# Low part of every second FFN weight chunk: an adding DMA onto a negated high part, in place of a VectorE subtraction

## The chip, the cores and the metric

The kernel runs on one core of one Trainium2 chip. The metric is the device time of one execution in microseconds (us). The engines are TensorE (PE, with its weight loads PEld), VectorE (DVE), ScalarE (ACT), GpSimd (POOL) and SyncE (SP); transfers run on 16 DMA engines that all queues share. Times of single steps come from one profiled execution, in which "L184" means line 184 of the kernel.

## What is computed

One decoder layer over 256 tokens of width 2048: a gated recurrent branch and a stick-breaking attention branch, merged, then a SwiGLU feed-forward block (FFN) and a gated per-layer embedding. The change touches only the weights of the FFN, the middle lines here:

```python
x = x + mix @ w_o
h = rmsnorm(x, g_ffn)
g, u = split(h @ w_ffn_gu, 2)          # w_ffn_gu: 2048 x 11264
x = x + (silu(g) * u) @ w_ffn_down     # w_ffn_down: 5632 x 2048
x = x + sigmoid(rmsnorm(x, g_ple) @ w_ple_gate) * (p @ w_ple_proj)
```

All values are float32. TensorE multiplies float32r, a shortened format, so every operand is carried as a high part, rounded to float32r, and a low part, the remainder. A product is high x high + high x low + low x high.

## The kernel before, in words

**Weights as a stream.** All weight matrices are packed in the order of use (`PLAN`) and cut into 690 chunks of at most eight 128x128 tiles; a full chunk is 128 x 1024 floats, 512 KB. `Stream` moves them through three stages. `dma_to` (L167) loads chunk j from device memory into one of four `w32` buffers, issued from SP. `split_to` makes the parts: ScalarE copies `w32` into `whi` (L183, rounding to float32r), VectorE subtracts `whi` from `w32` into `wlo` (L184). `whi` and `wlo` have four buffers each, so chunk j can be split only when TensorE has finished chunk j-4. `need` keeps the split three chunks ahead of the use and the loads four further.

**Use.** `dense` multiplies a block of chunks. A `wide` matmul (L366) takes a tile of `whi` against 512 columns, the activations' high and low parts side by side; a `low` matmul (L370) takes a tile of `wlo` against 256 columns, the high parts. In each chunk all eight of one kind run and then all eight of the other: low first in odd places of a block and in its last chunk, wide first in the others.

**The FFN.** Chunks 382 to 653, 272 of 690. `gu(q)` takes for each pair of rows a block of four chunks for the gate and four for the up projection; `dense_sum` adds the two column halves (ScalarE, then VectorE), a scaling, Silu and a product follow, and `split` writes the result's parts (L256 on ScalarE, L250 on VectorE). `down(q)` uses blocks of three chunks of six to eight tiles and adds into the residual on VectorE. The order is gu, gu, down, gu, down, gu, down, down. After the first block of the FFN and after the first of the last stage, a sum over all ones (L419) gives the norm.

**Order.** The program text gives every engine's instructions, and a list scheduler, which has a timeline of its own, decides the order in which they stand in each engine's queue. Each engine takes its queue strictly in order and waits at an instruction whose inputs or buffers aren't there yet.

Of the kernel before, what the change touches and what calls it, by code (L numbers as in the profile page):

```python
# [8 lines left out]
F32 = mybir.dt.float32  # L9
F32R = mybir.dt.float32r  # L10
AF = mybir.ActivationFunctionType
ALU = mybir.AluOpType

P = 128
# [111 lines left out]
PLAN = plan()  # L126
# [10 lines left out]
OFFS = []  # L137
# [11 lines left out]
class Stream:  # L149
# [23 lines left out]
    def split_to(self, n):  # L173
        n = min(n, len(CHUNKS))
        self.dma_to(n)
        while self.n_split < n:
            j = self.n_split
            i, a, b = CHUNKS[j]
            t = self.raw.pop(j)
            c = P * (b - a)  # L180
            hi = self.phl.tile([P, 1024], F32R, tag="whi", name=f"whi_{j}")
            lo = self.phl.tile([P, 1024], F32R, tag="wlo", name=f"wlo_{j}")
            self.hi_ins = self.nc.scalar.activation(hi[:, :c], t[:, :c], AF.Copy)  # L183
            self.lo_ins = self.nc.vector.tensor_tensor(lo[:, :c], t[:, :c], hi[:, :c].bitcast(F32), ALU.subtract)  # L184
            res = self.parts.setdefault(i, [])
            for x in range(b - a):
                s = slice(x * P, (x + 1) * P)
                res.append((hi[:, s], lo[:, s], hi, lo, x * P))
            self.n_split += 1
# [715 lines left out]
```

## Time and profile before

| | |
|---|---|
| Median of 3 runs (lowest to highest) | 1933.47 us (1933.33 to 1933.83) |
| The profiled execution, its own time | 1933.27 us |
| Its span, first to last instruction | 1931.5 us |
| Granted TensorE clock, mean | 0.999 |
| VectorE, ScalarE, share of the span | 67%, 57% |
| Read from device memory | 357.68 MB, 186 GB/s over the span |

The span is the stretch that the trace covers; the execution's own time is 1.8 us longer. "Busy" is time in which an engine works on an instruction; matmuls overlap, so TensorE's own busy time says that it never stood still, and the starts of its runs tell how long they really take. "Idle before" and the waits name what an engine stood still for.

### The profile page before, as it was taken

To read this page: it belongs to the slowest core of one execution; us is meant where nothing else is said; L and a number is where in the kernel's file an instruction comes from. 1 tells how busy PE (TensorE), PEld (TensorE's weight loads), DVE (VectorE), ACT (ScalarE), POOL (GpSimd) and SP (SyncE) were. 2 spreads that over 40 slices of the span, in tenths; PEclk is the share of its full clock that TensorE was granted. 3 is DMA by queue.
4 is the path that set the end of the run, shared out by engine and by line. 5 is a ranking of instruction groups with operands and counts; after the bars stand their busy time and mean duration, and the time that the engine had idled before them with its cause. 6 is when DMAs were issued, how large, how long until landed. Compare 5 with 4: busy or idle time off the path is not lost.

```text
span 1931.5 us, 28549 instructions
## 1 busy us (share of the span) xinstructions
PE 1923.7 (100%) x11126; PEld 1702.5 (88%) x11126; DVE 1293.2 (67%) x1848; ACT 1109.2 (57%) x1504; POOL 1.8 (0%) x8
## 2 busy tenths in 40 slices
PE   9999999999999999999999999999999999999998
PEld 8889889988888888888888888888888888888888
DVE  8787778665567777765666666666566665666775
ACT  7787778854466667674454544444344444444553
POOL 0000000000000000000000000000000000000000
PEclk9999999999999999999999999999999999999999
DMA  6556565566655555556666566666666566665664
GB/s 245 194 183 198 177 201 173 187 199 191 198 176 171 169 163 154 175 173 200 202 210 189 182 196 187 187 194 187 193 188 186 178 201 190 188 198 175 196 205 133
DMA packets 104391, 361.64 MB, mean 187 GB/s; under 512 B 11584, under 2 KB 13760, under 8 KB 104256
## 3 DMA queue, kind: packets, MB, share of 16 engines
q1 hardware_dynamic: 104112, 359.71, 58.8%
q8 instruction: 87, 1.43, 0.3%
q14 instruction: 48, 0.39, 0.1%
q10 hardware_dynamic: 144, 0.12, 0.0%
HBM read 357.68 MB, written 2.10 MB: 186 GB/s over the span
## 4 chain that ended last, share of the span: by engine, by line
PE 99%; ACT 1%; DVE 0%; issue 0%; ACTq 0%
PE ps L366 58%; PE ps L370 30%; PE ps L622 2%; PE ps L621 2%; PE ps L620 2%; PE ps L348 1%; PE ps L350 1%; PE ps L349 1%; PE ps L338 0%; PE ps L451 0%; ACT whi L183 0%; ACT T L256 0%; PE ps L602 0%; PE ps L601 0%; PE ps L339 0%; PE ps L419 0%
## 5 line engine op out<-in xcount | busy, mean ns | idle before, releaser
L184 DVE TENSOR_TENSOR wlo<-w,whi 128x1024 fp32r<-128x1024 f32 (+4 forms) x690 | 824.1, 1197 | 426.8 <-ACT whi L183 421.3
L183 ACT ACTIVATE whi<-w 128x1024 fp32r<-128x1024 f32 (+4 forms) x690 | 713.6, 1037 | 507.2 <-PE ps L366 373.8
L366 PE MATMUL ps<-B,whi 128*128 128x512 f32 x2528 | 611.0, 391 | 0.0
L366 PE MATMUL ps<-A,whi 128*128 128x512 f32 x2400 | 585.6, 391 | 0.0
L366 PEld LDWEIGHTS ps<-B,whi 128*128 128x128 f32 x2528 | 464.0, 188 | 89.1
L366 PEld LDWEIGHTS ps<-A,whi 128*128 128x128 f32 x2400 | 438.6, 188 | 83.3
L370 PEld LDWEIGHTS ps<-B,wlo 128*128 128x128 f32 x2528 | 325.9, 191 | 13.1
L370 PE MATMUL ps<-B,wlo 128*128 128x256 f32 x2528 | 330.1, 283 | 0.0
L370 PEld LDWEIGHTS ps<-A,wlo 128*128 128x128 f32 x2400 | 312.5, 191 | 14.4 <-DVE wlo L184 1.2
L370 PE MATMUL ps<-A,wlo 128*128 128x256 f32 x2400 | 320.0, 283 | 0.8 <-DVE wlo L184 0.8
L256 ACT ACTIVATE T<-ps 128x256 f32<-128x256 f32 x242 | 79.3, 380 | 209.6 <-PE ps L366 209.6
L250 DVE TENSOR_TENSOR T<-ps,T 128x256 f32<-128x256 f32 x242 | 92.0, 419 | 129.6 <-ACT T L256 129.5
L256 ACT ACT_TABLE_LOAD x65 | 83.4, 1283 | 5.1 <-DVE ze L250 2.7
L256 ACT ACTIVATE T<-T 128x512 f32<-128x512 f32 (+2 forms) x116 | 69.7, 602 | 20.9 <-DVE T L250 20.0
L250 DVE TENSOR_TENSOR T<-T,rstd 128x256 f32<-128x256 f32 x194 | 75.0, 418 | 2.5 <-ACT rstd L256 2.3
L250 DVE TENSOR_TENSOR C<-ps,C 128x256 f32<-128x256 f32 x176 | 63.1, 417 | 15.1 <-PE ps L366 13.4
L250 DVE TENSOR_TENSOR T<-T,T 128x512 f32<-128x512 f32 (+2 forms) x109 | 70.3, 646 | 2.5 <-ACT T L256 2.2
L622 PE MATMUL ps<-whi,A 128*128 128x512 f32 x128 | 49.8, 389 | 0.0
L621 PE MATMUL ps<-wlo,A 128*128 128x512 f32 x128 | 49.8, 389 | 0.0
L620 PE MATMUL ps<-whi,A 128*128 128x512 f32 x128 | 48.9, 389 | 0.0
L253 DVE SCALAR_TENSOR_TENSOR T<-T,prm_sb,T 128x255 f32<-128x255 f32 (+3 forms) x74 | 34.6, 507 | 8.0 <-ACT T L256 7.9
L348 PE MATMUL ps<-X,whi 128*128 128x256 f32 x140 | 39.6, 283 | 0.0
(138 smaller groups left out, 868.5 us busy)
## 6 DMA issues: line engine op xcount, KB each, us to landing
w<-in_w_dram SPq DMA_DIRECT2D x588, 512.0 KB, 3.7
w<-in_w_dram SPq DMA_DIRECT2D x80, 448.0 KB, 3.4
w<-in_w_dram SPq DMA_DIRECT2D x16, 384.0 KB, 3.0
C<-in_xT_dram SPq DMA_DIRECT2D x16, 256.0 KB, 4.0
out_dram<-T SPq DMA_DIRECT2D x16, 128.0 KB, 3.8
w<-in_w_dram SPq DMA_DIRECT2D x4, 320.0 KB, 3.4
w<-in_w_dram SPq DMA_DIRECT2D x2, 256.0 KB, 4.2
T<-in_pT_dram SPq DMA_DIRECT2D x1, 256.0 KB, 4.7
```

What stands on the lines that cost most here:

```text
L183: self.hi_ins = self.nc.scalar.activation(hi[:, :c], t[:, :c], AF.Copy)
L184: self.lo_ins = self.nc.vector.tensor_tensor(lo[:, :c], t[:, :c], hi[:, :c].bitcast(F32), ALU.subtract)
L250: nc.vector.tensor_tensor(o, a, b, op)
L253: nc.vector.scalar_tensor_tensor(o, a, s, b, op0, op1)
L256: nc.scalar.activation(o, i, f, **kw)
L348: nc.tensor.matmul(o, wt[0], xh, start=start, stop=False)
L349: nc.tensor.matmul(o, wt[0], xl, start=False, stop=False)
L366: nc.tensor.matmul(pss[e], wt[0], rhs(xs, k), start=(k == 0), stop=(k == n - 1))
L370: nc.tensor.matmul(pss[e][:, :256], wt[1], rhs(xs, k)[:, :256], start=False, stop=False)
L620: nc.tensor.matmul(ps, xh, wh, start=(k == 0), stop=False)
L621: nc.tensor.matmul(ps, xh, wl, start=False, stop=False)
L622: nc.tensor.matmul(ps, xl, wh, start=False, stop=(k == KD - 1))
```

## The change

For FFN chunks (`gu`, `dn`) with an odd number, 136 of the 272, `wlo` is made in two steps instead of one. ScalarE writes the negated high part into `wlo` (L186), and a DMA issued from GpSimd (L187) reads the chunk's weights a second time from device memory and adds them in place. VectorE's subtraction (L184 before, L189 after) remains for the other chunks.

```diff
             self.hi_ins = self.nc.scalar.activation(hi[:, :c], t[:, :c], AF.Copy)
-            self.lo_ins = self.nc.vector.tensor_tensor(lo[:, :c], t[:, :c], hi[:, :c].bitcast(F32), ALU.subtract)
+            if PLAN[i][0][0] in ("gu", "dn") and j % 2:
+                src = self.w[OFFS[j]:OFFS[j] + P * c].rearrange("(p c) -> p c", p=P)
+                self.nc.scalar.activation(lo[:, :c], hi[:, :c].bitcast(F32), AF.Copy, scale=-1.0)
+                self.nc.gpsimd.dma_start(lo[:, :c], src, accum_op=ALU.add)
+            else:
+                self.lo_ins = self.nc.vector.tensor_tensor(lo[:, :c], t[:, :c],
+                                                           hi[:, :c].bitcast(F32), ALU.subtract)
```

Queue by queue, the built program has 136 instructions fewer on VectorE, 136 copies more on ScalarE (and one table load more), and 136 DMAs on GpSimd, whose queue held nothing in this part before. SP's queue is the same, instruction by instruction. Up to the FFN all queues agree.

From chunk 383 on the scheduler also orders TensorE's and ScalarE's work anew. In a stretch of `gu`, which repeats every eight chunks, TensorE's order is this (hi396 is the eight wide matmuls of chunk 396, lo396 its eight low ones, "hi402 x4" four of them):

```
before: hi396 lo396 | lo397 hi397 | hi398 lo398 | lo399 hi399 | hi400 lo400 | lo401 hi401 | hi402 lo402 | lo403 hi403 | hi404 ...
after:  hi396 lo396 | hi398 lo398 | lo397 hi397 | lo399 hi399 | hi400 lo400 | hi402 x4 | lo401 hi401 | hi402 x4 lo402 | lo403 hi403 | hi404 ...
```

and ScalarE's order after is (evac: the two copies out of PSUM; neg397: the new copy that writes -whi into `wlo` of chunk 397):

```
whi398, neg397, Silu, whi399, neg399, whi400, whi401, neg401, evac, whi402, whi403, split, neg403, whi404, evac, whi405, whi406, neg405, Silu, ...
```

Each adding DMA waits for its neg; the first low matmul of an odd chunk waits for that DMA.

## The prediction

> **What bounds the kernel now.** I read the busy times and the chain of waits first, then TensorE's waits, and then two long windows inside the FFN.
>
> ```profile
> span 1931.5 us, 28549 instructions
> PE 1923.7 (100%) x11126; PEld 1702.5 (88%) x11126; DVE 1293.2 (67%) x1848; ACT 1109.2 (57%) x1504; POOL 1.8 (0%) x8
> ...
> PE 99%; ACT 1%; DVE 0%; issue 0%; ACTq 0%
> ```
>
> ```profile
> PE ps L451 <- DVE T L302: 2.0, 1, 2.0
> PE ps L370 <- DVE wlo L184: 0.8, 1, 0.8
> ```
>
> ```profile
> 1150.00:1400.00 250.00, 250.00 (x1439) 220.93 (x1438) 151.11 (x204) 114.57 (x141) 0.00 (x0) 1.00 0.62 190
> 1400.00:1780.00 380.00, 380.00 (x2183) 335.54 (x2182) 234.72 (x327) 171.49 (x211) 0.00 (x0) 1.00 0.60 188
> 10.00:12.00 2.00, 2.00 (x11) 1.62 (x10) 2.00 (x4) 1.91 (x5) 0.00 (x0) 1.00 1.03 414
> 12.00:14.00 2.00, 2.00 (x16) 1.88 (x15) 2.00 (x5) 2.00 (x5) 0.00 (x0) 1.00 1.04 415
> ```
>
> The columns of a window are its length, the busy time and count of PE, PEld, DVE, ACT and POOL, the granted clock, the share of the DMA engines, and GB/s. TensorE bounds the kernel: 99% of the chain, 1923.7 of 1931.5 us, and in the FFN it is never idle, at a granted clock of 1.00. It waited for the low parts once, 0.8 us in all. VectorE, which the change relieves, works 151.1 of 250 us there; its work is hidden. So there is almost nothing to win: at most that 0.8 us, and 7.8 us of TensorE's idle time in the whole span, nearly all outside the FFN. What decides is whether the new way of making `wlo` still comes in time.
>
> **How long TensorE takes for a chunk.** Matmuls overlap, so I take the starts of TensorE's runs:
>
> ```profile
> 1204.66 3.82 PE L366 MATMUL ps<-B,whi 128*128 128x512 f32 x16
> 1208.31 2.08 PE L370 MATMUL ps<-B,wlo 128*128 128x256 f32 x16
> 1210.22 2.00 PE L366 MATMUL ps<-B,whi 128*128 128x512 f32 x8
> ```
>
> Sixteen wide matmuls take 1208.31 - 1204.66 = 3.65 us, sixteen low ones 1.91. A chunk of eight tiles is 1.83 + 0.96 = 2.78 us, eight chunks 22.2. The window agrees: 250 us / 1439 matmuls x 16 = 2.78.
>
> **What is removed.** 136 subtractions on VectorE, and with them the waits of SP's load queue on them:
>
> ```profile
> L184 DVE TENSOR_TENSOR wlo<-w,whi 128x1024 fp32r<-128x1024 f32 (+4 forms) x690 | 824.1, 1197 | 426.8 <-ACT whi L183 421.3
> ```
>
> ```profile
> SPq L167 <- DVE wlo L184: 592.9, 256, 4.1
> ```
>
> 136 x 1.2 = 163 us of VectorE's time go. It was beside TensorE's work, so this brings 0 to 0.8 us (the one wait above). A `w32` buffer of an odd chunk comes free some 1.2 us earlier; TensorE waits for no load now, so this brings nothing either.
>
> **What is added on ScalarE.** 136 copies of the size of L183's:
>
> ```profile
> L183 ACT ACTIVATE whi<-w 128x1024 fp32r<-128x1024 f32 x199 | 210.8, 1059 | 192.8 <-PE ps L366 146.7 <-issue 45.4 <-ACT A L256 0.8
> ...
> L256 ACT ACTIVATE A<-T 128x512 fp32r<-128x512 f32 x14 | 8.8, 632 | 6.9 <-DVE T L250 6.9
> ```
>
> 136 x 1.06 = 144 us. The first window holds 250 / 2.78 = 90 chunks, so 45 copies: 114.6 + 47.7 = 162 of 250 us, 65%. ScalarE doesn't become the bound; the cover is its 192.8 us of waiting before L183. But the copy stands in the path of the low part, and in its queue ahead of the next `whi`.
>
> **The wait that is added.** The first low matmul of an odd chunk now waits for whi, neg and the adding DMA in turn. Behind that matmul stands all of TensorE's work, and behind TensorE the buffers of the next chunks. On GpSimd only the next adding DMA is queued behind one that waits. How long may the DMA take? From the changed order, four odd chunks repeat in every eight (even chunks: their subtraction is as before). Each neg stands behind a whi that needs the buffer of the chunk four earlier, so the clock starts when TensorE ends that chunk's wide matmuls:
> - chunk 401: whi401 needs the end of hi397. Until lo401 TensorE has chunks 399 and 400 and four of hi402, 2 x 2.78 + 0.91 = 6.47 us. ScalarE takes 2 x 1.06 = 2.12. Left for the DMA: **4.3 us**.
> - chunk 403: from the end of hi399 chunks 400, 401 and 402, 8.34 us, less 2.12 and 0.63 for the split: 5.6.
> - chunk 399: from hi395 three chunks, 8.34 - 2.12 = 6.2.
> - chunk 397: neg stands behind whi398, which needs hi394; lo394 and three chunks, 0.96 + 8.34 - 2.12 = 7.2.
>
> So the tightest place, one in eight chunks, comes 272 / 8 = 34 times in the FFN. In `down`, whose blocks are ordered differently, about a quarter of the odd chunks have 4.3 us or less too, so I use the same count there. If L, the time from neg to the landed sum, is over 4.3, TensorE waits L - 4.3 at each tight place; that wait is given to chunks 399 and 403 as well, so they add nothing. Above L = 7.2 chunk 397 is late too, and then the eight chunks take two links of 2.12 + L, two chunks and four wide matmuls: 2 x (2.12 + L) + 2 x 2.78 + 0.91 = 2L + 10.7 against 22.2.
>
> **L, the unknown.** No row of before shows an adding DMA or one from GpSimd. The nearest are the plain loads of the same chunks, from SP, in the whole span and then in its first 30 us, where the DMA engines were full (the 10 to 14 us windows above: share 1.03, 415 GB/s):
>
> ```profile
> w<-in_w_dram SPq DMA_DIRECT2D x588, 512.0 KB, 3.7
> w<-in_w_dram SPq DMA_DIRECT2D x80, 448.0 KB, 3.4
> w<-in_w_dram SPq DMA_DIRECT2D x16, 384.0 KB, 3.0
> ```
>
> ```profile
> w<-in_w_dram SPq DMA_DIRECT2D x13, 512.0 KB, 5.5
> ```
>
> Low bound: a plain load, 3.7 us, which fits everywhere. Between 384 and 512 KB the landing grows by 0.7 us for 128 KB, so of the 3.7 some 2.8 go with the size and 0.9 do not. An adding transfer has to fetch two operands, the weights and the old content of `wlo`. If each passes like a load, L = 0.9 + 2 x 2.8 = 6.5. Issue from GpSimd isn't free: I add 0.5, about two of POOL's eight instructions (1.8 / 8 = 0.23 us each in the first fence), and take **L = 7.0**. High bound: if the written sum is a third pass in series, 0.9 + 3 x 2.8 + 0.5 = 9.8. I take the middle one because two operands can't be avoided, while a write in a plain load is already in its 2.8.
>
> The Trainium skill, page "Collectives: The Full Stack", section "Part 3: Why 7× under link rate — side-by-side accounting", says that a reduction in the DMA engines runs at half the rate of a copy because each chunk needs two source reads, not because the add costs anything. By it L would be the 6.5 us above and the loss 75 us; without it, at a copy's price, nothing is lost. The trace of before holds no adding DMA that could bear it out.
>
> **The sum.** Against the profiled execution's own 1933.27 us (span 1931.5, and 1.8 around it; the median 1933.47 is 0.01% away): 34 x (7.0 - 4.3) = +92 us, less at most 0.8. **2025 us**, 4.7% slower. Other values: L = 3.7 gives 1932.5 to 1933.3, 5.5 gives +41 (1974), 8 gives 34 x (26.7 - 22.2) = +153 (2086), 9.8 gives 34 x (30.3 - 22.2) = +275 (2209), 10 gives +289 (2222).
>
> **The rivals.**
> 1. *The DMA comes in time, and nothing changes* (not slower). The place is lo401 and its like, the point L = 4.3 us. For it: a plain load of the same bytes lands in 3.7, and the DMA engines are only 0.60 to 0.62 busy. Against it: that leaves 0.6 us for the second operand and the issue, and the same load took 5.5 us once the engines were full. Time 1933, within the 0.2% (3.9 us) that a measurement of this kernel can tell from no change. The Trainium skill, page "DMA: Bandwidth & Descriptors", section "Anatomy of one DMA — SWDGE (gpsimd) path", gives a plain DMA from GpSimd 2.0 us + bytes / 436e3, which for 512 KB is an estimate of 3.2 us; by that rule, and if the add is free, this rival would hold. No row of before has a DMA from GpSimd.
> 2. *L is beyond 8 us*, because the add is done in series, or because the DMA must share each engine with the loads. Then two links in eight chunks are late: 2086 to 2222 us. For it: the landing already grows from 3.7 to 5.5 when the engines fill up. Against it: a waiting TensorE also slows the loads, which leaves the adding DMA more room.
> 3. *The DMA engines become the bound.* The loads move 188 GB/s, and every second chunk again would be 94 for each pass. Two passes give 188 + 188 = 376, under the 415 shown at the start; three give 470 and four 564. The FFN lies between the first and the last L419:
>
> ```profile
> L419 PE MATMUL ps<-T,ones x8: 377/378/382, 1099.8 to 1832.4; 128*128 128x256 f32 x8
> ```
>
> It takes 1832.4 - 1099.8 = 733 us, so three passes cost 733 x (470 / 415 - 1) = 97 us (2030), four 263 (2196). For it: the share of 0.60 is more than half. Against it: it needs a third pass.
>
> Faster by over 3.9 us would need more than the 0.8 us that the removed work ever cost TensorE; only a gain of TensorE's new order that no row shows could do it.
>
> **How the numbers follow.** Forecast (L from 4.4 to 8, 1937 to 2086 us): 0.60. Rival 1: 0.12. Rival 2: 0.14. Rival 3: 0.12. Faster: 0.02. The range goes from 1940 (L = 4.5) to 2222 (L = 10, beyond the bound of 9.8, and rival 3's four passes within it); below lie rival 1 and faster, 0.14, above some 0.06. Slower by over 0.2%: 0.60 + 0.14 + 0.12 = 0.86; within: 0.12; faster: 0.02.
>
> **What would show it.** In the changed profile TensorE should wait at L370 for the DMA into `wlo`, some 2.7 us a time and about 34 times or more, beginning at chunk 383; the DMAs at L187 should land 6 to 8 us after their issue; VectorE should lose about 163 us of busy time and ScalarE gain 144; the share of the DMA engines in the FFN should rise from 0.6 towards 0.9 (376 of 415 GB/s), and nothing should change until some 15 us before the first L419 row, 1099.8 us, where the first block of the FFN stands (4 x 2.78 = 11.1 us). If the landing is under 4.3 us and no such wait stands there, rival 1 is right. If the DMA share is near 1.0 and SP's loads land late as well, it is rival 3. I would be wrong in the whole if TensorE waits for something else, ScalarE's `whi` for instance, which the copies now delay, or if the chunks before 382 change.

## The result and the profile after

The changed kernel takes 2049.90 us (2047.74 to 2050.56, three runs) against 1933.47: ratio 1.0599, 95% interval 1.0575 to 1.0623. That is 116.4 us more, where +92 was forecast. The page of after, busy times and chain of waits:

```profile
span 2046.0 us, 28830 instructions
PE 1958.5 (96%) x11126; PEld 1714.0 (84%) x11126; DVE 1139.2 (56%) x1712; ACT 1239.9 (61%) x1640; POOL 119.8 (6%) x144
...
PE 71%; DMA 21%; issue 6%; ACT 1%; DVE 1%; SPq 0%; POOL 0%; POOLq 0%; DVEq 0%; ACTq 0%
```

VectorE lost 154 us and ScalarE gained 131, near the 163 and 144 of the sum, and neither matters. The chain, 99% TensorE before, now runs through the adding DMAs for a fifth of its length. The weight loads' and the matmuls' waits, the adding DMAs' times (L187), and the sum over ones that marks the FFN, now at L425:

```profile
PEld ps L376 <- DMA wlo<-in_w_dram: 101.3, 73, 3.3
...
PE ps L376 <- DMA wlo<-in_w_dram: 79.9, 61, 3.1
```

```profile
L187 POOL DMA_DIRECT2D wlo<-in_w_dram x136: 865/865/1013, 1085.6 to 1930.6; - x136
...
DMA to landing us min/median/max: 5.3/7.5/9.6
```

```profile
L425 PE MATMUL ps<-T,ones x8: 377/378/382, 1098.1 to 1947.1; 128*128 128x256 f32 x8
```

The FFN takes 1947.1 - 1098.1 = 849.0 us instead of 732.6: all of the loss lies in it. A matmul's weight load goes ahead of it and is what stands at the wait; it waited 73 times, 1.4 us in the mean, 101.3 us in all. The remaining 15 us or so come beside a lower clock (the windows' columns are as in the prediction):

```profile
1100.00:1400.00 300.00, 266.25 (x1458) 228.46 (x1457) 101.48 (x159) 166.47 (x207) 38.93 (x45) 0.98 0.92 238
1400.00:1780.00 380.00, 346.27 (x1887) 297.01 (x1886) 130.83 (x215) 204.34 (x239) 52.80 (x61) 0.97 0.93 245
```

A clock of 0.98 over 300 us and 0.97 over 380 is about 17 us (an estimate) if TensorE's work stretches with it. The share of the DMA engines is 0.92 to 0.93: by this view alone one could as well say that the DMA engines are full. That had to be told apart.

### The profile page after: what moved, and what is told of

Its sections match the earlier page's. It is cut to its first block, busy times and chain, and to the rows that moved or that the text cites. A ratio compares the mean times of both kernels' runs of the same rounds, so it can differ in the third digit from the quotient of the medians.

```text
span 2046.0 us, 28830 instructions
## 1 busy us (share of the span) xinstructions
PE 1958.5 (96%) x11126; PEld 1714.0 (84%) x11126; DVE 1139.2 (56%) x1712; ACT 1239.9 (61%) x1640; POOL 119.8 (6%) x144
## 3 DMA queue, kind: packets, MB, share of 16 engines
q0 software_dynamic: 19584, 69.21, 19.0%
## 4 chain that ended last, share of the span: by engine, by line
PE 71%; DMA 21%; issue 6%; ACT 1%; DVE 1%; SPq 0%; POOL 0%; POOLq 0%; DVEq 0%; ACTq 0%
PE ps L372 39%; PE ps L376 22%; DMA wlo<-in_w_dram 20%; PE ps L626 1%; PE ps L628 1%; PE ps L627 1%; PE ps L354 1%; PE ps L356 1%; PE ps L355 1%; ACT wlo L186 1%; ACT whi L183 0%; PE ps L344 0%; DMA w<-in_w_dram 0%; DVE A L259 0%; DVE wlo L189 0%
## 5 line engine op out<-in xcount | busy, mean ns | idle before, releaser
L189 DVE TENSOR_TENSOR wlo<-w,whi 128x1024 fp32r<-128x1024 f32 (+3 forms) x554 | 662.7, 1199 | 514.5 <-ACT whi L183 506.4
L372 PE MATMUL ps<-B,whi 128*128 128x512 f32 x2528 | 630.9, 397 | 0.0
L372 PEld LDWEIGHTS ps<-B,whi 128*128 128x128 f32 x2528 | 470.8, 192 | 90.1
L376 PEld LDWEIGHTS ps<-B,wlo 128*128 128x128 f32 x2528 | 335.5, 192 | 99.2 <-DMA wlo<-in_w_dram 83.5
L376 PE MATMUL ps<-B,wlo 128*128 128x256 f32 x2528 | 352.7, 287 | 67.7 <-DMA wlo<-in_w_dram 67.5
L376 PEld LDWEIGHTS ps<-A,wlo 128*128 128x128 f32 x2400 | 311.4, 191 | 31.3 <-DMA wlo<-in_w_dram 17.8
L376 PE MATMUL ps<-A,wlo 128*128 128x256 f32 x2400 | 322.7, 283 | 13.5 <-DMA wlo<-in_w_dram 12.3
L187 POOL DMA_DIRECT2D wlo<-in_w_dram x136 | 117.9, 867 | 1811.0 <-ACT wlo L186 1649.4
L186 ACT ACTIVATE wlo<-whi 128x1024 fp32r<-128x1024 f32 (+1 forms) x136 | 140.6, 1034 | 14.3 <-PE ps L376 11.5
```

The source lines that it names most:

```text
L186: self.nc.scalar.activation(lo[:, :c], hi[:, :c].bitcast(F32), AF.Copy, scale=-1.0)
L187: self.nc.gpsimd.dma_start(lo[:, :c], src, accum_op=ALU.add)
L372: nc.tensor.matmul(pss[e], wt[0], rhs(xs, k), start=(k == 0), stop=(k == n - 1))
L376: nc.tensor.matmul(pss[e][:, :256], wt[1], rhs(xs, k)[:, :256], start=False, stop=False)
```

## The experiments

The lead is how many chunks the split runs ahead of the use; the landing is the time from a DMA's issue until its data are in place. Four theories. **A**: TensorE waits because the path from a free buffer to a landed sum is longer than the lead; it is a matter of latency. **B**: the DMA engines are full. **C**: ScalarE's 136 copies delay the parts. **E**: the scheduler's new order makes the tight places. The last experiments add two: **D**, an adding DMA costs the same whatever its size, and **C2**, each adding DMA costs a wait of its own.

| run | time, us | ratio to before (95%) | landing, median us | weight loads' wait for it, us |
|---|---|---|---|---|
| changed kernel | 2049.90 | 1.0599 (1.0575 to 1.0623) | 7.5 | 101.3 |
| e3, copy kept, sum on VectorE | 1933.56 | 0.9999 (0.9990 to 1.0009) | | |
| e5b, both added beside, TensorE doesn't wait | 1933.49 | 0.9999 (0.9989 to 1.0008) | 8.4 | |
| e1, one buffer more, lead of four | 1940.30 | 1.0037 (1.0025 to 1.0048) | 7.7 | 7.8 |
| e8, before with a lead of four | 1931.38 | 0.9989 (0.9980 to 0.9998) | | |
| e2, plain DMA from GpSimd | 1950.93 | 1.0087 (1.0070 to 1.0103) | 4.9 | 17.0 |
| e4, half of the columns | 1965.35 | 1.0160 (1.0145 to 1.0174) | 6.0 | 27.5 |
| e10, a quarter | 1934.91 | 1.0008 (0.9998 to 1.0017) | 5.0 | 2.2 |
| e7, one of four chunks | 1992.76 | 1.0306 (1.0292 to 1.0321) | 6.3 | 50.3 |
| e9, change in program order | 2066.25 | 1.0682 (1.0659 to 1.0704) | 7.2 | 113.0 |
| e11, before in program order | 1940.37 | 1.0035 (1.0022 to 1.0048) | | |
| e5, adding DMAs beside, not tied | 1987.37 | 1.0278 (1.0263 to 1.0294) | 8.4 | |

**e3: the copy without the DMA.**

```diff
-                self.nc.gpsimd.dma_start(lo[:, :c], src, accum_op=ALU.add)
+                self.nc.vector.tensor_tensor(lo[:, :c], t[:, :c], lo[:, :c].bitcast(F32), ALU.add)
```

> The changed kernel with the negated copy kept on ScalarE, but the sum made on VectorE, no DMA. Theory A: 1930 to 1938 us, as before, since the copy's 1.06 us fits in the lead. Theory C, the copies delay whi: a good part of the loss stays, over 1960 us. Theory B as A.

1933.56 us against 1933.70 for before in the same series: ScalarE's copies cost nothing. Theory C falls.

**e5 and e5b: the DMAs without the wait.** Both add to the kernel before. e5 has the second line only; `side` is one of two scratch tiles in turn, and the lines that make them and `src` are left out here:

```diff
+                self.nc.scalar.activation(side[:, :c], hi[:, :c].bitcast(F32), AF.Copy, scale=-1.0)
+                self.nc.gpsimd.dma_start(side[:, :c], src, accum_op=ALU.add)
```

> The kernel before, with the adding DMAs of the change beside it: 136 of the same size and at the same places, into two scratch tiles that nothing reads (SBUF from two T buffers and one X buffer). Nothing waits for them, the DMA engines carry what they carry in the changed kernel. Theory A: 1931 to 1945 us, loads landing in 5 to 6 us instead of 3.7, a granted clock near 1.00. Theory B, the engines are full: the loads come late, over 1980 us with TensorE waiting at L183 and L184's results. If the clock falls to 0.97 here too, it is the transfers and not TensorE's waiting that lower it.

> The kernel before, and beside it what the change adds, at the change's own places: ScalarE's negated copy into one of two scratch tiles and the adding DMA onto it, which nothing reads; the low parts come from VectorE as before (SBUF from two T buffers and one X buffer). Theory A, the loss is TensorE's wait for the landed sum: 1930 to 1942 us, although the DMA engines carry the same bytes, and a granted clock of 1.00. Theory B, the full DMA engines themselves: over 1970 us, with TensorE waiting for VectorE's low parts because the loads come late.

e5's 1987 us are what theory B forecast, but e5 missed its aim: without the copy nothing ties the DMAs to the FFN, so GpSimd issued them from the start, each as soon as a scratch tile was free. Its DMAs' durations and first and last start, a window of its first part, and the largest wait of ScalarE from 100 to 590 us:

```profile
L187 POOL DMA_DIRECT2D side<-in_w_dram x136: 862/862/1216, 4.3 to 593.4; - x136
```

```profile
100.00:300.00 200.00, 187.65 (x1130) 166.60 (x1130) 141.14 (x209) 146.65 (x205) 38.86 (x45) 1.00 1.05 291
```

```profile
ACT whi L183 <- DMA w<-in_w_dram: 139.2, 90, 3.7
```

That is one adding DMA in (593.4 - 4.3) / 135 = 4.4 us beside the loads, and there theory B's effect exists: ScalarE waits 139.2 us for late weights, TensorE is busy for 187.65 of 200 us, and the run is 54 us slower. e5b puts the same DMAs at the change's own places, from 1086.3 to 1820.7 us, one in 734.4 / 135 = 5.4 us; its windows in the FFN:

```profile
1100.00:1400.00 300.00, 300.00 (x1727) 265.09 (x1726) 183.01 (x245) 195.58 (x233) 46.60 (x54) 1.00 1.02 282
1400.00:1780.00 380.00, 380.00 (x2184) 335.54 (x2183) 235.26 (x327) 237.96 (x283) 60.46 (x70) 1.00 1.02 283
```

More bytes per second than in the changed kernel (282 against 238 to 245), a share of 1.02, a landing of 8.4 us, and TensorE busy for 680 of 680 us: 1933.49. Nothing reads the sums; only ScalarE's next copy into a scratch tile waited for them, 9 times, 3.3 us in all. So neither the copies nor the transfers cost anything by themselves; in the changed kernel it is the wait. The clock is 1.00 here and 0.97 where TensorE stands still, so it isn't the transfers that lower it.

**e1 and e8: more lead.** The lines of e1 (e8 has the same); not shown is that one X and two T buffers fewer make the room, as in e5 and e5b.

```diff
-    phl = ctx.enter_context(tc.tile_pool(name="phl", bufs=4))
+    phl = ctx.enter_context(tc.tile_pool(name="phl", bufs=5))
-    S_ = Stream(nc, w, p32, phl, 4, 3)
+    S_ = Stream(nc, w, p32, phl, 3, 4)
```

> The changed kernel with five whi and wlo buffers and the split four chunks ahead instead of three (SBUF for it comes from two T buffers and one X buffer). Theory A, the lead is too short: each place gains one chunk of 2.78 us, so the tightest has 7.1 us against some 7.8 from neg to landed sum; TensorE's waits for the adding DMA fall from 101 us to under 30, the FFN from 849 us to 740 to 770, the time to 1940 to 1965 us. Theory B, the DMA engines are full: at 0.92 to 0.94 over 849 us, the same packets in 733 us would be a share of 1.07, so the FFN stays over 790 us and the time over 1985 us. Theory C, ScalarE's copies delay whi: no change, 2040 to 2060 us.

> The kernel before with five whi and wlo buffers and the split four chunks ahead, as the changed kernel had them in the first look, without the change. In that look the part behind the FFN was 5.5 us shorter than before. If that came from the lead, 1926 to 1930 us, and the true loss that the change has left with a lead of four is 10 to 14 us; if it came from chance or the change, 1932 to 1936 us.

The weight loads' wait and a window of the FFN, both of e1:

```profile
PEld ps L376 <- DMA wlo<-in_w_dram: 7.8, 8, 2.6
```

```profile
1400.00:1780.00 380.00, 378.63 (x2171) 333.68 (x2170) 150.52 (x250) 239.50 (x277) 60.47 (x70) 1.00 1.02 280
```

The landing is no shorter (7.7 us), but the waits fall from 101.3 to 7.8 us and the time from 2049.90 to 1940.30. Of theory B's floor of 1985 us nothing is seen. With five buffers a buffer also serves odd and even chunks in turn, so that only every second use of it has a DMA; no run separates that from the longer lead. e8 is the fair comparison: with a lead of four but without the change the kernel takes 1931.38 us, 2.3 us under before (ratio just clear of 1) and the fastest of all; that lies between the two times expected for it, so whether the lead brought the gain stays open. Given its lead, the change still costs 8.9 us and wins nothing.

**e9 and e11: the order.** The argument `schedule_with_timeline_sim=True` is dropped, in the change and in before.

> The changed kernel with the scheduler's own timeline switched off: TensorE's queue then has the order of before (each odd chunk low first right behind its even neighbour) and no chunk is passed over. Theory A, the loop over four buffers: 2.78 us of matmuls, 2.1 for whi and neg, some 0.5 of hops and 7.5 for the landing are 12.9 us whatever the order, against the 11.1 that four chunks take; the FFN takes 733 + 68 x 1.8 = 855 us, the changed kernel 849. Theory E, my step: the tight place of 4.3 us that the new order makes is what costs: with 6.2 us at every chunk the FFN falls under 825 us.

> The kernel before with the scheduler's own timeline switched off, as the reference for the other: TensorE is fed all the time in the FFN, which takes 733 us as before; the whole 1930 to 1950 us.

e9's FFN takes 858 us, 855 expected; against e11 (FFN 738 us) the change costs 126 us, so the scheduler's new order didn't cause the loss (theory E falls); at most it saved a little. e9 is needed for that: in the stretches looked at (from 1290, 1420 and 1600 us on) the traces of e1, e3 and e5b show TensorE in the order of before, sixteen wide and sixteen low matmuls in turn, and e10's does so nearly, so these runs took the tight places away as well. e2 and e4 have orders of their own. e9's chain of waits shows the loop bare (start, length, what):

```profile
1297.17 7.44 DMA wlo<-in_w_dram
1304.61 0.04 issue
1304.65 1.22 PE ps L376 x8
1305.87 1.85 PE ps L372 x8
1307.73 0.02 issue
1307.75 1.07 ACT whi L183
1308.82 0.02 issue
1308.84 1.07 ACT wlo L186
1309.91 0.28 issue
1310.19 6.75 DMA wlo<-in_w_dram
```

A sum lands, its chunk's low and wide matmuls run (3.07 us, the first low one slower after a wait), the wide ones free a `whi` buffer, ScalarE fills it and writes the negation, GpSimd issues 0.28 us later, and the next sum of the same buffer begins: 1310.19 - 1297.17 = 13.02 us, of which 5.58 aren't the DMA. TensorE needs 4 x 2.78 = 11.1 for the four chunks that share the loop. So the landing may take **11.1 - 5.6 = 5.5 us**. In the changed kernel the chain runs through the same kind of loop twice, from the wait at 1306.08 us to the one at 1331.94:

```profile
1306.08 1.22 PE L376 MATMUL ps<-B,wlo 128*128 128x256 f32 x8 [1.92 <-DMA wlo<-in_w_dram]
...
1318.74 1.21 PE L376 MATMUL ps<-B,wlo 128*128 128x256 f32 x8 [0.91 <-DMA wlo<-in_w_dram]
...
1331.94 0.38 PE L376 MATMUL ps<-B,wlo 128*128 128x256 f32 x1 [1.80 <-DMA wlo<-in_w_dram]
```

These are 25.9 us for eight chunks, with two waits to each eight, against 22.2.

**e2, e4, e10, e7: the landing and its limit.** e2 drops `accum_op=ALU.add`, so it leaves out the sum: `wlo` then holds the weights themselves. e4 gives the first half of the columns to ScalarE's copy and the DMA, the rest to VectorE; e10 has `c // 4` in place of `c // 2`. e7 changes one chunk in four. The lines of e4:

```diff
-                self.nc.scalar.activation(lo[:, :c], hi[:, :c].bitcast(F32), AF.Copy, scale=-1.0)
-                self.nc.gpsimd.dma_start(lo[:, :c], src, accum_op=ALU.add)
+                h = c // 2
+                self.nc.scalar.activation(lo[:, :h], hi[:, :h].bitcast(F32), AF.Copy, scale=-1.0)
+                self.nc.gpsimd.dma_start(lo[:, :h], src[:, :h], accum_op=ALU.add)
+                self.nc.vector.tensor_tensor(lo[:, h:c], t[:, h:c], hi[:, h:c].bitcast(F32), ALU.subtract)
```

and of e7:

```diff
-            if PLAN[i][0][0] in ("gu", "dn") and j % 2:
+            if PLAN[i][0][0] in ("gu", "dn") and j % 4 == 3:
```

> The changed kernel with the DMA from GpSimd as a plain load into wlo, no addition (so the low parts of these chunks are the weights themselves, not the remainder). Theory A: with one operand instead of two the landing falls from 7.5 to about 5 us and the time per packet to about half, the waits to some 20 to 40 us, the time to 1945 to 1980 us; the rest is what the issue from GpSimd costs. Theory B: the share of the DMA engines falls to about 0.8 and the time to about 1935 to 1950 us. If the addition costs nothing, as against a plain load, landing and time stay at 7.5 and 2050 us.

> The changed kernel with the adding DMA, and the negated copy, on the first half of an odd chunk's columns alone; VectorE subtracts the other half. Theory A, a loop over the four buffers (2.78 us of matmuls, 1.06 for whi, 0.6 for the shorter copy, 0.3 to the issue, and the landing) that must be under four chunks, 11.1 us: the landing falls to about 5 us, the loop to 9.8, TensorE's waits to under 20 us, the time to 1933 to 1950 us. Theory D, the cost is per DMA whatever its size (issue, landing): landing stays at 7 or more and the time over 2020 us.

> As the kernel with the adding DMA on half of the columns, but on a quarter, VectorE doing three quarters. If of the landing (7.6 us for 512 KB, 6.0 for 256 KB) some 4.4 us don't depend on the size, 128 KB land in 5.2 us; neg takes about 0.45 us, the loop 2.78 + 1.06 + 0.45 + 0.5 + 5.2 = 10.0 us and the tight place of 4.3 us alone is late: TensorE's waits fall from 27 to under 15 us, the time to 1938 to 1953 us. If the landing is by what the prediction took, 0.9 + 0.5 and the rest by size, it is near 2.8 us and the time 1931 to 1936 us.

> The changed kernel with only the chunks whose number leaves 3 after division by 4 changed, 68 of the 136, one set of whi and wlo buffers. Theory A: that buffer's loop is as before, so with a landing of 6 to 7.5 us it takes 11.2 to 12.7 us of the 11.1 there are: 68 waits of 0.1 to 1.6 us, 1940 to 2040 us, more than half of the loss if the landing stays at 7.5. Theory B, the load of the DMA engines (share then near 0.8): 1933 to 1945 us. Theory C2, every adding DMA costs its own wait: half of the loss, 1985 to 1995 us.

The plain DMA lands in 4.9 us, under the limit of 5.5, and only stragglers are waited for, 17.0 us. (e2's time alone says little against theory B, whose range ended at 1950 us.) The landing by size, from the lists of DMA issues: e2's plain DMA, then the adding one of the changed kernel, e4 and e10:

```profile
wlo<-in_w_dram POOLq DMA_DIRECT2D x112, 512.0 KB, 5.0
```

```profile
wlo<-in_w_dram POOLq DMA_DIRECT2D x112, 512.0 KB, 7.6
```

```profile
wlo<-in_w_dram POOLq DMA_DIRECT2D x112, 256.0 KB, 6.0
```

```profile
wlo<-in_w_dram POOLq DMA_DIRECT2D x112, 128.0 KB, 4.9
```

The expected 5 us for half were wrong, and so were both times expected for e4; theory D, a cost per DMA whatever its size, is half right. Between 128 and 512 KB the landing grows by only 2.7 us, so some 4 us don't depend on the size. This is an estimate: the load on the DMA engines falls with the size too, from a share of 0.92 to 0.85 and 0.78, and in e7, at 0.81, 512 KB land in 6.2 us. With half the columns the shorter copy (0.62 us instead of 1.03) moves the limit to about 5.9 us: a median of 6.0 is at it, 27.5 us of waits. With a quarter (copy 0.41 us, limit some 6.1) 5.0 is under it, and the loss is within 0.2%. For e10 1938 to 1953 us had been expected with this landing, because the tight place of 4.3 us was still counted on; its order has hardly any, and 2.2 us of waits are left. e7 has half as many DMAs, a share of 0.81 and a landing of 6.3 us, over the limit still: 68 DMAs, 50.3 us of waits, half of the loss. That number alone would also fit theory C2, a wait of its own for each DMA; e10, with all 136 DMAs and 2.2 us of waits, speaks against it.

## Why the prediction was right

**Right: the bound, and what the change removes.** TensorE bounds the kernel, VectorE's subtractions were hidden, and nothing was won. In e3 and e5b the hidden work is worth nothing either way. Up to the FFN nothing changed.

**Right: the added wait is the mechanism.** TensorE waits at L376 for the DMA into `wlo` and for little else, as the last part of the prediction asked, and the adding DMAs land within the 6 to 8 us that it named. e5b and e1 show it: the same transfers without the wait, or with a longer lead, and the loss is gone or nearly so.

**Mis-sized: L.** Taken: 7.0 us from neg to the landed sum. Measured: 0.28 us to the issue and 7.5 to the landing, 7.8. That passes the 7.2 of chunk 397, from which the prediction counts two late links in eight chunks (its second rival begins at 8). Its formula for them, 2L + 10.7, gives 26.3 us per eight chunks, where 25.9 are seen above. So the right L would not have given the right time: 34 x (26.3 - 22.2) is +139, and +116 was measured, with some 17 of it beside the lower clock.

**Right by luck: how L was composed.** The prediction split a load into 0.9 us fixed and 2.8 by size, and doubled the latter. The runs show some 4 us that don't depend on the size (the estimate above). What does grow with size is doubled nevertheless: from GpSimd's queue (packets, MB, share of 16 engines) in the changed kernel's page and then in e2's,

```profile
q0 software_dynamic: 19584, 69.21, 19.0%
```

```profile
q0 software_dynamic: 19584, 69.21, 10.7%
```

an adding packet takes 0.190 x 16 x 2046.0 / 19584 = 0.318 us and a plain one of e2 0.107 x 16 x 1950.8 / 19584 = 0.171, a factor of 1.9. The Trainium skill's page "Collectives: The Full Stack", section "Part 3: Why 7× under link rate — side-by-side accounting", has a reduction at half a copy's rate for its two source reads. The factor of 1.9 agrees with it, but a halved rate is no doubled landing here: 7.5 us against 4.9.

**Wrong: the step on the places.** For an L of up to 7.2 the prediction counted 34 tight places with 4.3 us and said that the wait there "is given to chunks 399 and 403 as well, so they add nothing". It took chunk 401's place for the bound because the scheduler's order makes it the shortest. The bound is the loop over four buffers: a short place borrows from the next, but the loop leaves a mean of 5.5 us for the landing, and it is passed twice in eight chunks. e9 has the order of before, without such a place, and e10 nearly so: with a landing of 7.2 us e9 loses as much as the changed kernel, with 5.0 us e10 loses nothing. So 73 waits of 1.4 us stand where 34 of 2.7 were forecast; the products, 101 and 92 us, are near each other because the two errors cancel, which is luck too.

**Missed: the clock.** The prediction's sum has no term for it. It was 0.97 to 0.98 in the FFN, some 17 us, a part of the difference between 92 and 116. That waits and clock add up so can be set against other profiled executions: e4 had 27.5 us of waits at a clock of 1.00 and lost 1961.1 - 1933.3 = 27.8 us; e7 had 50.3 us at 0.99, which over 680 us is an estimate of 6.8 more, and lost 1990.2 - 1933.3 = 56.9.

**Rivals.** Rival 1 (in time) is what happens with a quarter of the columns. The 2.0 us + bytes / 436e3 of the Trainium skill's page "DMA: Bandwidth & Descriptors", section "Anatomy of one DMA — SWDGE (gpsimd) path", by which, with a free addition, it would have held, gives an estimate of 3.2 us for 512 KB. The plain DMA of e2 took 5.0 beside the loads, so here the measurement decides against it. Rival 3 (the DMA engines) is refuted by e5b at this rate and shown by e5 at a rate a quarter higher. The reason given against it, that it needs a third pass, wasn't tested by a run of its own; an adding packet's 1.9 times a plain one's time looks like two passes, not three.

What stays open: why the clock falls. It does so in runs in which TensorE waits often and not in e5b, but no run varied the waits alone, and their sum doesn't set it: the same stretch has 0.99 in e9 with 113.0 us of waits, 0.97 to 0.98 in the changed kernel with 101.3.

## What to carry to other kernels

When a buffered stream gets a step with a long latency, write down the loop through one buffer (use, free, refill, latency, use) and set it against the number of buffers times the time of one use; here the loop was the bound, not the tight place in the order. A high share of the DMA engines doesn't say that they are the bound: add the same transfers with nobody waiting for them, at the same places, and see. Work that is hidden is worth nothing to move, so first ask which wait of the bounding engine it ends.

## What was not expected of the hardware

- The DMA engines' share went to 1.02 at 282 GB/s without any loss (e5b), and to 1.05 at 291 with 54 us of loss (e5).
- An adding DMA holds GpSimd for 0.862 to 0.865 us, be it the whole chunk, a half or a quarter (medians of the changed kernel, e4 and e10); a plain one holds it for 0.527 (e2).
- 128 KB added from GpSimd land in 4.9 us (e10), about as long as 512 KB by a plain DMA from it (5.0, e2).
